# The last normalisation of a two-layer streaming encoder: mean taken off first, weight and bias last

## The chip, the cores and the metric

The kernel runs on one core of one Trainium2 chip. The core has a matrix engine (PE, with its weight loads shown as PEld), a vector engine (DVE), a scalar engine (ACT), a third elementwise engine (POOL, GpSimd) and a queue engine (SP), which issues most transfers. The metric is the time of one execution in microseconds of device time. Less is better. Before the change the median of three runs is 2924.94 us (2924.41 to 2925.33).

## The reference

One inference step of a two-layer encoder over 256 prompt frames and 32 sample frames, 288 together, each of 2048 channels. Layer 0 mixes tokens by a gated MLP, layer 1 by retention; after each comes a SwiGLU feed-forward. Every sublayer ends in a residual and a normalisation over the 2048 channels of a frame. The change touches the very last of the four:

```python
def layer_norm(x, g, b):
    xf = x.astype(jnp.float32)
    mu = jnp.mean(xf, axis=-1, keepdims=True)
    var = jnp.mean(jnp.square(xf - mu), axis=-1, keepdims=True)
    y = (xf - mu) * lax.rsqrt(var + LN_EPS) * g.astype(jnp.float32) + b.astype(jnp.float32)
    return y.astype(x.dtype)

def trunk(x, ...):
    for i in range(DEPTH):
        ...
        x = layer_norm(ALPHA * x + h, ln_mix_g[i], ln_mix_b[i])
        x = layer_norm(ALPHA * x + swiglu(x, w_ffn_in[i], w_ffn_out[i]), ln_ffn_g[i], ln_ffn_b[i])
    return x, ...
```

## The kernel before

Activations are held transposed: a tile is 128 channels (partitions) by 288 frames, and `y` has KT = 16 such tiles side by side. Weights come in blocks of 128 by 128, eight to a chunk of 512 KB, on SP's queue; ACT and DVE split every chunk into a rounded part and the rest (`split`, lines 363 to 365), and PE makes three products for each block (`step`, lines 91 to 98). The blocks follow one another in the order in which PE uses them. PE's order is the order of the program; the other engines' instructions are put in order by a scheduler when the kernel is built.

The last feed-forward ends with 16 output tiles, one after the other, 22 blocks each. When one is done, `PostNorm.last` (line 210) adds it to `y` on DVE (line 215). A rough mean `c`, taken from the first tile in `center`, is subtracted from every tile (line 252), so that the later squares stay small. `sums` (line 250) squares the tile on ACT (line 254) and adds tile and square to two running sums on DVE (lines 257 and 258). For the last normalisation (`self.out` is set) it also multiplies the tile by its weight on ACT (line 264).

The 16th tile isn't added to the sums: `stats` (line 266) multiplies the sums (line 275) and the last tile and its square (line 278) by a constant matrix of 1/2048 on PE, which leaves the mean `m1` and the mean square `m2` of every frame in two PSUM banks, on all partitions alike. Then come, one after the other: the weight of the last tile (281), the square of the mean (285), the variance `v` (286), a first value of its inverse root by Ln and Exp (292, 293), one Newton step of three instructions on DVE (`newton`, lines 165 to 168), which gives the factor `a`, its copy into a PSUM bank `ap` (296), and the offset `b = -mean * a` (297).

After that the tiles are finished in pairs. `scale` (line 301) multiplies a pair by the factor, on DVE with `ap`, or on POOL with `a` for pairs 4 and 10. `shift` (line 305) forms on ACT, for each tile, `b` times the weight plus the bias in a buffer `wide` (line 308), and adds the two to the pair, on DVE or POOL (line 309). Eight stores of a pair each, 288 KB, follow on SP's queue in the order 0, 2, 6, 4, 8, 12, 10, 14 (line 322); each waits until its pair is done.

Buffers: PSUM has four banks for products (`acc`) and four others (`aux`); SBUF has three buffers for incoming weight chunks (tag `raw`).

Of the kernel before, what the change touches and what calls it, by code (L numbers as in the profile page):

```python
# [8 lines left out]

F32 = mybir.dt.float32  # L10
F32R = mybir.dt.float32r
I32 = mybir.dt.int32
AF = mybir.ActivationFunctionType
ALU = mybir.AluOpType
PSUM = bass.MemoryType.PSUM
PE = mybir.EngineType.PE

P = 128
D = 2048
KT = D // P  # L20
NP = 256
NS = 32
NT = NP + NS
# [9 lines left out]
LN_EPS = 1e-5  # L33
GN_EPS = 1e-6
CB = 8
# [7 lines left out]
class Core:  # L43
# [47 lines left out]
    def step(self, ps, w, k, m, x, first, last):  # L91
        mm = self.nc.tensor.matmul
        hi, lo = self.blk(w, k, m)
        xh, xl = x
        n = xh.shape[-1]
        mm(ps[:, :n], hi, xh, start=first, stop=False)  # L96
        mm(ps[:, :n], hi, xl, start=False, stop=False)  # L97
        mm(ps[:, :n], lo, xh, start=False, stop=last)  # L98
# [59 lines left out]
def rsqrt(nc, out, v, t):  # L158

    nc.vector.tensor_scalar(out.bitcast(I32), v.bitcast(I32), -0.5, float(0x5F3759DF), ALU.mult, ALU.add)  # L160
    for _ in range(3):
        newton(nc, out, out, v, t)


def newton(nc, out, r, v, t):
    nc.vector.scalar_tensor_tensor(t, r, -0.5, r, ALU.mult, ALU.mult)
    nc.vector.tensor_tensor(t, t, v, ALU.mult)
    nc.vector.scalar_tensor_tensor(out, t, 1.5, r, ALU.add, ALU.mult)


class PostNorm:
# [38 lines left out]
    def last(self, m, ps, first_part=False):  # L210
        nc, lnp, gi = self.nc, self.lnp, self.gi
        if first_part:
            self.part(m, ps)
        else:
            nc.vector.tensor_tensor(self.y[:, m, :], ps[:, :NT], self.y[:, m, :], ALU.add)
        if self.n == 0:
            self.s = lnp.tile([P, 2, NT], F32, tag="sums", name=f"sums{gi}")
            nc.gpsimd.memset(self.s, 0.0)
            if self.out is not None:
                self.core.tc.keep_in_program_order(nc.scalar.preload_act_table_set("natural_log_exp_and_others"))  # L220
            else:
                gb = self.cst["ln"][:, gi, :, :].rearrange("p a k -> p k a")
                nc.scalar.copy(self.xh[:, :, NT:], gb)
                nc.vector.tensor_tensor(self.xl[:, :, NT:], gb, self.xh[:, :, NT:].bitcast(F32), ALU.subtract)
            r = self.tmp("cen", F32R)
            nc.scalar.copy(r, self.y[:, m, :])
            self.core.after(2, lambda: self.center(r))
        self.n += 1
        if self.c is None:
            self.wait.append(m)  # L230
        else:
            self.sums(m)
        if self.n == KT:
            if self.out is None:
                self.parts = [[self.tmp(f"s{i}{j}", F32R) for j in range(2)] for i in range(2)]
                for i, (hi, lo) in enumerate(self.parts):
                    split(nc, hi, lo, self.s[:, i, :])
            self.core.after(1 if self.out is not None else 2, lambda: self.stats(m))

    def center(self, r):  # L240

        nc = self.nc
        ps = self.core.bank(f"cen{self.gi}")
        nc.tensor.matmul(ps[:, :NT], self.cst["one_r"], r, start=True, stop=True)
        self.c = self.lnp.tile([P, NT], F32, tag="cen", name=f"cens{self.gi}")
        nc.scalar.mul(self.c, ps[:, :NT], float(KT))
        for q in self.wait:
            self.sums(q)

    def sums(self, m):  # L250
        nc, d = self.nc, self.y[:, m, :]
        nc.vector.tensor_tensor(d, d, self.c, ALU.subtract)
        sq = self.tmp(f"sq{m}")
        nc.scalar.activation(sq, d, AF.Square)
        self.sq = sq
        if self.n < KT or self.out is None:
            nc.vector.tensor_tensor(self.s[:, 0, :], self.s[:, 0, :], d, ALU.add)
            nc.vector.tensor_tensor(self.s[:, 1, :], self.s[:, 1, :], sq, ALU.add)
        if self.out is None:
            g = self.gain(m)  # L260
            nc.scalar.mul(self.xh[:, m, :NT], d, g)
            nc.vector.scalar_tensor_tensor(self.xl[:, m, :NT], d, g, self.xh[:, m, :NT].bitcast(F32), ALU.mult, ALU.subtract)
        elif self.n < KT:
            nc.scalar.mul(d, d, self.gain(m))

    def stats(self, m):
        nc, core, gi = self.nc, self.core, self.gi
        one = self.cst["one2048"]
        st = [core.bank(f"m{i}_{gi}") for i in range(2)]
        for i in range(2):  # L270
            if self.out is None:
                for j, r in enumerate(self.parts[i]):
                    nc.tensor.matmul(st[i][:, :NT], self.cst["one_r"], r, start=j == 0, stop=j == 1)
            else:
                nc.tensor.matmul(st[i][:, :NT], one, self.s[:, i, :], start=True, stop=False)
        if self.out is not None:
            for i, r in enumerate((self.y[:, m, :], self.sq)):
                nc.tensor.matmul(st[i][:, :NT], one, r, start=False, stop=True)
        m1, m2 = st[0][:, :NT], st[1][:, :NT]
        if self.out is not None:  # L280
            nc.scalar.mul(self.y[:, m, :], self.y[:, m, :], self.gain(m))
        v, t = self.tmp("v"), self.tmp("t")
        self.a = a = self.lnp.tile([P, NT], F32, tag="a", name=f"a{gi}")
        self.b = b = self.lnp.tile([P, NT], F32, tag="b", name=f"b{gi}")
        nc.scalar.activation(t, m1, AF.Square)
        nc.vector.scalar_tensor_tensor(v, m2, LN_EPS, t, ALU.add, ALU.subtract)
        if self.out is None:
            rsqrt(nc, a, v, t)
            nc.vector.scalar_tensor_tensor(b, m1, -1.0, a, ALU.mult, ALU.mult)
            return  # L290
        r = self.tmp("r")
        nc.scalar.activation(t, v, AF.Ln)
        nc.scalar.activation(r, t, AF.Exp, scale=-0.5)
        ap = core.bank("ap")[:, :NT]
        newton(nc, a, r, v, t)
        nc.scalar.copy(ap, a)
        nc.vector.scalar_tensor_tensor(b, m1, -1.0, a, ALU.mult, ALU.mult)
        pool = (4, 10)
        row = lambda k: self.y[:, k:k + 2, :]

        def scale(k):
            eng, f = (nc.gpsimd, a) if k in pool else (nc.vector, ap)
            eng.tensor_tensor(row(k), row(k), f.unsqueeze(1).broadcast_to([P, 2, NT]), ALU.mult)

        def shift(k):
            u = self.wide(k // 2)
            for i in range(2):
                nc.scalar.activation(u[:, i, :], b, AF.Identity, bias=self.bias(k + i), scale=self.gain(k + i))
            (nc.gpsimd if k in pool else nc.vector).tensor_tensor(row(k), row(k), u, ALU.add)

        for k in pool:
            scale(k)
        ks = [k for k in range(0, KT, 2) if k not in pool]
        scale(ks[0])
        for k, nxt in zip(ks, ks[1:] + [None]):
            if nxt is not None:
                scale(nxt)
            shift(k)
            if k in (2, 8):
                shift(k + 2)  # L320
        for k in (0, 2, 6, 4, 8, 12, 10, 14):
            nc.sync.dma_start(self.out[:, k:k + 2, :], row(k))

    def norm(self, k):
        nc, d = self.nc, self.y[:, k:k + 2, :]
# [37 lines left out]
def split(nc, hi, lo, f):  # L363
    nc.scalar.copy(hi, f)  # L364
    nc.vector.tensor_tensor(lo, f, hi.bitcast(F32), ALU.subtract)  # L365
# [426 lines left out]
def hybrid_step(ctx, tc, ins, outs):  # L792
    nc = tc.nc
    ctx.enter_context(tc.manual_schedule(engines={PE}))
    core = Core(ctx, tc, ins["wpack"])
# [112 lines left out]
```

## Time and profile before

| what | value |
|---|---|
| median of three runs | 2924.94 us |
| the profiled execution, its own time | 2923.75 us |
| its span, first to last instruction | 2922.0 us |
| mean granted clock of PE | 0.997 |
| PE busy | 99% of the span |
| DVE, ACT, POOL busy | 59%, 43%, 5% |
| start of the last product of the feed-forward | 2900.84 us |
| first store of the result issued | 2910.34 us |
| last store issued | 2918.49 us |
| a store, from issue to landing | 2.1 to 2.6 us, median 2.3 |

All times of the trace are microseconds from the first instruction. A row of the timeline gives start, duration, engine, line, operation, what is written and read with shapes, a count where equal rows are merged, and in brackets how long the engine stood idle before and what ended that. A row of a group gives busy time and the mean duration of one in ns, and the idle time before. A duration holds the whole life of one instruction; where the next doesn't depend on it, it may start some tenths of a microsecond before that ends, so that the distance of two starts is what a row of such instructions costs.

### The profile page before, as it was taken

The numbers are of one execution on the slowest core, as the hardware profiler recorded it, in microseconds if no ns is written. First come the engines' busy times: TensorE is split into PE (matmuls) and PEld (weight loads), VectorE is DVE, ScalarE is ACT, GpSimd is POOL, SyncE is SP. The second block draws the span as 40 slices with busy tenths as digits, with TensorE's granted clock in tenths as the row PEclk, the third lists the DMA queues.
The fourth block names the chain that finished last, engine by engine and source line by source line (L and its number), as shares of the span: only waits on it lengthen the run. The fifth ranks groups of instructions, "written<-read, shape, count | busy, mean of one in ns | idle before, by whom it ended". The sixth has DMA issues, their size and how long they took to land.

```text
span 2922.0 us, 51538 instructions
## 1 busy us (share of the span) xinstructions
PE 2899.8 (99%) x21576; PEld 2885.3 (99%) x21576; DVE 1712.9 (59%) x2489; ACT 1256.8 (43%) x1676; POOL 141.6 (5%) x236
## 2 busy tenths in 40 slices
PE   9999999999999999999999999999999999999997
PEld 9999999999999999999999999999999999999997
DVE  5667865444444456787755566767864444444455
ACT  5444544333333344564443344445553333333344
POOL 1100000000000000012200111200000000000000
PEclk9999999999999999999999999999999999999998
DMA  8644445555544545557654566655545554455553
GB/s 281 211 161 159 159 166 166 166 165 163 165 165 166 166 159 169 187 185 233 223 185 166 185 214 202 222 183 166 160 158 173 166 166 163 164 165 166 166 166 112
DMA packets 147161, 516.16 MB, mean 177 GB/s; under 512 B 18080, under 2 KB 21168, under 8 KB 146768
## 3 DMA queue, kind: packets, MB, share of 16 engines
q1 hardware_dynamic: 132704, 474.28, 49.3%
q0 software_dynamic: 14224, 38.59, 4.4%
q8 instruction: 169, 2.77, 0.4%
q14 instruction: 64, 0.52, 0.1%
HBM read 487.63 MB, written 25.17 MB: 175 GB/s over the span
## 4 chain that ended last, share of the span: by engine, by line
PE 98%; DVE 1%; ACT 0%; DMA 0%; SPq 0%; issue 0%; DVEq 0%; ACTq 0%
PE af_in L97 13%; PE af_in L96 13%; PE af_in L98 13%; PE ab_in L97 7%; PE ab_in L96 7%; PE ab_in L98 7%; PE af_out L96 6%; PE af_out L98 6%; PE af_out L97 6%; PE ab_out L98 2%; PE ab_out L96 2%; PE ab_out L97 2%; PE aa_in L96 2%; PE aa_in L97 2%; PE aa_in L98 2%; PE aa_out L96 1%
## 5 line engine op out<-in xcount | busy, mean ns | idle before, releaser
L365 DVE TENSOR_TENSOR wlo<-raw,whi 128x1024 fp32r<-128x1024 f32 (+1 forms) x894 | 1085.9, 1216 | 937.3 <-ACT whi L364 933.3
L364 ACT CAST whi<-raw 128x1024 fp32r<-128x1024 f32 (+1 forms) x894 | 931.1, 1043 | 1479.9 <-PE af_in L97 370.5
L97 PE MATMUL af_in<-xl,whi 128*128 128x288 f32 (+1 forms) x2816 | 833.0, 296 | 0.0
L96 PE MATMUL af_in<-xh,whi 128*128 128x288 f32 (+1 forms) x2816 | 832.9, 296 | 0.0
L98 PE MATMUL af_in<-xh,wlo 128*128 128x288 f32 (+1 forms) x2816 | 831.8, 295 | 0.0
L97 PEld LDWEIGHTS af_in<-xl,whi 128*128 128x128 f32 x2816 | 532.1, 189 | 0.0
L98 PEld LDWEIGHTS af_in<-xh,wlo 128*128 128x128 f32 x2816 | 531.6, 189 | 0.0
L96 PEld LDWEIGHTS af_in<-xh,whi 128*128 128x128 f32 x2816 | 531.1, 189 | 0.0
L97 PE MATMUL ab_in<-xl,whi 128*128 128x288 f32 (+1 forms) x1536 | 454.4, 296 | 0.7 <-DVE xl L365 0.7
L96 PE MATMUL ab_in<-xh,whi 128*128 128x288 f32 (+1 forms) x1536 | 454.9, 296 | 0.0
L98 PE MATMUL ab_in<-xh,wlo 128*128 128x288 f32 (+1 forms) x1536 | 453.6, 295 | 0.0
L96 PE MATMUL af_out<-hh,whi 128*128 128x288 f32 x1408 | 416.0, 295 | 0.0
L97 PE MATMUL af_out<-hl,whi 128*128 128x288 f32 x1408 | 415.1, 295 | 0.0
L98 PE MATMUL af_out<-hh,wlo 128*128 128x288 f32 x1408 | 414.4, 294 | 0.0
L97 PEld LDWEIGHTS ab_in<-xl,whi 128*128 128x128 f32 x1536 | 290.3, 189 | 2.0 <-DVE xl L365 0.9
L96 PEld LDWEIGHTS ab_in<-xh,whi 128*128 128x128 f32 x1536 | 289.6, 189 | 1.0
L98 PEld LDWEIGHTS ab_in<-xh,wlo 128*128 128x128 f32 x1536 | 289.9, 189 | 0.0
L98 PEld LDWEIGHTS af_out<-hh,wlo 128*128 128x128 f32 x1408 | 264.9, 188 | 0.0
L97 PEld LDWEIGHTS af_out<-hl,whi 128*128 128x128 f32 x1408 | 264.2, 188 | 0.0
L96 PEld LDWEIGHTS af_out<-hh,whi 128*128 128x128 f32 x1408 | 263.9, 187 | 0.0
L96 PE MATMUL aa_in<-xh,whi 128*128 128x288 f32 x512 | 152.7, 298 | 1.1 <-ACT whi L364 1.1
L98 PE MATMUL aa_in<-xh,wlo 128*128 128x288 f32 x512 | 151.5, 296 | 0.7 <-DVE wlo L365 0.7
(237 smaller groups left out, 2976.6 us busy)
## 6 DMA issues: line engine op xcount, KB each, us to landing
raw<-in_wpack_dram SPq DMA_DIRECT2D x886, 512.0 KB, 3.4
v_room<-tv POOLq DMA_DIRECT2D x32, 144.0 KB, 4.7
of<-o_room POOLq DMA_DIRECT2D x32, 144.0 KB, 4.5
vw<-v_room POOLq DMA_DIRECT2D x8, 512.0 KB, 5.4
out_st_s_dram<-sso POOLq DMA_DIRECT2D x16, 256.0 KB, 2.8
out_st_p_dram<-so POOLq DMA_DIRECT2D x16, 256.0 KB, 5.3
o_room<-to POOLq DMA_DIRECT2D x8, 512.0 KB, 3.8
y<-in_xT_dram SPq DMA_DIRECT2D x8, 288.0 KB, 6.7
```

The lines of the kernel that those rows point to most:

```text
L96: mm(ps[:, :n], hi, xh, start=first, stop=False)
L97: mm(ps[:, :n], hi, xl, start=False, stop=False)
L98: mm(ps[:, :n], lo, xh, start=False, stop=last)
L364: nc.scalar.copy(hi, f)
L365: nc.vector.tensor_tensor(lo, f, hi.bitcast(F32), ALU.subtract)
```

## The change

Only the last normalisation changes. The multiplication of each tile by its weight in the loop (264 and 281) goes. When the 15th tile has come (`last`, n = 15), a buffer of tag `raw` is taken for two matrices of 128 by 128: an identity, made on POOL, and one that is -1 in its first row and 0 elsewhere. The rough mean is subtracted from tile 15 then, before its last product is added. The two sums over the first 15 tiles are split into a rounded part and the rest, and are multiplied by the rounded constant matrix on PE.

What follows the statistics is a new function, `finish`, in an order written out by hand for DVE, ACT and POOL; SP's queue is still put in order by the scheduler. ACT copies the mean into SBUF. The mean is taken off first: on PE for tiles 6, 7, 12 and 13 (an identity product of the tile plus one of the -1 row with the mean, in four PSUM banks `off`), on POOL for pairs 4, 8 and 10, on DVE for pairs 0, 2 and 14. `v` and the Newton step lie in PSUM banks, and the factor ends in `ap` without a copy; a copy of it goes to SBUF as `a`. The tiles are scaled by it, on POOL for its pairs, else on DVE. Weight and bias come last, in one instruction for each tile: on DVE for tiles 10, 11, 13, 14 and 15, on ACT for the others. Tile 12 is stored singly on ACT's queue and tile 13 singly on SP's; the others go in pairs.

```diff
@@ last
+        if self.out is not None and self.n == KT - 1:
+            room = self.core.wp.tile([P, CB * P], F32, tag="raw", name="centring", bufs=3)
+            self.ident, self.minus = room[:, :P], room[:, P:2 * P]
+            make_identity(nc, self.ident)
+            nc.gpsimd.memset(self.minus, 0.0)
+            nc.gpsimd.memset(self.minus[:1, :], -1.0)
+            d = self.y[:, KT - 1, :]
+            nc.vector.tensor_tensor(d, d, self.c, ALU.subtract)
...
+        if self.n == (KT if self.out is None else KT - 1):
+            self.parts = [[self.tmp(f"s{i}{j}", F32R) for j in range(2)] for i in range(2)]
+            for i, (hi, lo) in enumerate(self.parts):
+                split(nc, hi, lo, self.s[:, i, :])
@@ sums
-        nc.vector.tensor_tensor(d, d, self.c, ALU.subtract)
+        if self.out is None or self.n < KT:
+            nc.vector.tensor_tensor(d, d, self.c, ALU.subtract)
...
-        elif self.n < KT:
-            nc.scalar.mul(d, d, self.gain(m))
@@ stats
-                nc.tensor.matmul(st[i][:, :NT], one, self.s[:, i, :], start=True, stop=False)
+            for j, r in enumerate(self.parts[i]):
+                nc.tensor.matmul(st[i][:, :NT], self.cst["one_r"], r, start=j == 0, stop=j == 1 and self.out is None)
...
-            nc.scalar.mul(self.y[:, m, :], self.y[:, m, :], self.gain(m))
...
+    def finish(self, m1, m2):
+        nc, core, a, mean = self.nc, self.core, self.a, self.b
+        mm = nc.tensor.matmul
+        ap = core.bank("ap")[:, :NT]
+        v = core.accum("fin")[:, :NT]
+        t, r = self.tmp("t"), self.tmp("r")
+        pool = (4, 8, 10)
+        copied = (6, 7, 12, 13)
+        late = (10, 11, 13, 14, 15)
+        row = lambda k: self.y[:, k:k + 2, :]
+        off = {k: (core.bank if i == 3 else core.accum)(f"off{k}")[:, :NT] for i, k in enumerate(copied)}
+
+        def pair(k, op, vec, gp):
+            eng, f = (nc.gpsimd, gp) if k in pool else (nc.vector, vec)
+            eng.tensor_tensor(row(k), row(k), f.unsqueeze(1).broadcast_to([P, 2, NT]), op)
+
+        center = lambda k: pair(k, ALU.subtract, m1, mean)
+
+        def scale(k):
+            if k in copied:
+                for i in (k, k + 1):
+                    nc.vector.tensor_tensor(self.y[:, i, :], off[i], a, ALU.mult)
+            else:
+                pair(k, ALU.mult, ap, a)
+
+        def affine(k, n=2, queue=None):
+            for i in range(k, k + n):
+                d = self.y[:, i, :]
+                if i in late:
+                    nc.vector.tensor_scalar(d, d, self.gain(i), self.bias(i), ALU.mult, ALU.add)
+                else:
+                    nc.scalar.activation(d, d, AF.Identity, bias=self.bias(i), scale=self.gain(i))
+            (queue or nc.sync).dma_start(self.out[:, k:k + n, :], self.y[:, k:k + n, :])
+
+        with core.tc.manual_schedule(engines=FINISH):
+            nc.scalar.activation(t, m1, AF.Square)
+            nc.scalar.copy(mean, m1)
+            for k in copied:
+                mm(off[k], self.ident, self.y[:, k, :], start=True, stop=False)
+                mm(off[k], self.minus, mean, start=False, stop=True)
+            for k in pool:
+                center(k)
+            nc.vector.scalar_tensor_tensor(v, m2, LN_EPS, t, ALU.add, ALU.subtract)
+            nc.scalar.activation(t, v, AF.Ln)
+            nc.scalar.activation(r, t, AF.Exp, scale=-0.5)
+            center(0)
+            nc.vector.scalar_tensor_tensor(ap, v, -0.5, r, ALU.mult, ALU.mult)
+            nc.vector.tensor_tensor(ap, ap, r, ALU.mult)
+            nc.vector.scalar_tensor_tensor(ap, ap, 1.5, r, ALU.add, ALU.mult)
+            scale(0)
+            nc.scalar.copy(a, ap)
+            for k in pool:
+                scale(k)
+            center(2)
+            affine(0)
+            scale(6)
+            affine(6)
+            scale(2)
+            affine(4)
+            affine(2)
+            center(14)
+            scale(12)
+            affine(8)
+            scale(14)
+            affine(14)
+            affine(10)
+            affine(12, 1, nc.scalar)
+            affine(13, 1)
```

The removed part of `stats` and the old functions `scale` and `shift` with their loop are in the listing above.

More of the change, by code (lines that the diff above doesn't have):

```diff
@@ L8 @@
 from concourse._compat import with_exitstack
+from concourse.masks import make_identity
 F32 = mybir.dt.float32
@@ L16 @@
 PE = mybir.EngineType.PE
+FINISH = {mybir.EngineType.DVE, mybir.EngineType.Activation, mybir.EngineType.Pool}
 P = 128
@@ L232, in last @@
             self.sums(m)
+        if self.n == (KT if self.out is None else KT - 1):
+            self.parts = [[self.tmp(f"s{i}{j}", F32R) for j in range(2)] for i in range(2)]
+            for i, (hi, lo) in enumerate(self.parts):
+                split(nc, hi, lo, self.s[:, i, :])
         if self.n == KT:
[L234 to L237, printed above, removed]
             self.core.after(1 if self.out is not None else 2, lambda: self.stats(m))
@@ L270, in stats @@
         for i in range(2):
[L271 to L274, printed above, removed]
-                nc.tensor.matmul(st[i][:, :NT], one, self.s[:, i, :], start=True, stop=False)
+            for j, r in enumerate(self.parts[i]):
+                nc.tensor.matmul(st[i][:, :NT], self.cst["one_r"], r, start=j == 0, stop=j == 1 and self.out is None)
         if self.out is not None:
@@ L279, in stats @@
         m1, m2 = st[0][:, :NT], st[1][:, :NT]
-        if self.out is not None:
-            nc.scalar.mul(self.y[:, m, :], self.y[:, m, :], self.gain(m))
-        v, t = self.tmp("v"), self.tmp("t")
         self.a = a = self.lnp.tile([P, NT], F32, tag="a", name=f"a{gi}")
         self.b = b = self.lnp.tile([P, NT], F32, tag="b", name=f"b{gi}")
+        if self.out is not None:
+            self.finish(m1, m2)
+            return
+        v, t = self.tmp("v"), self.tmp("t")
         nc.scalar.activation(t, m1, AF.Square)
@@ L286, in stats @@
         nc.vector.scalar_tensor_tensor(v, m2, LN_EPS, t, ALU.add, ALU.subtract)
[L287 to L293, printed above, removed]
-        ap = core.bank("ap")[:, :NT]
-        newton(nc, a, r, v, t)
-        nc.scalar.copy(ap, a)
-        nc.vector.scalar_tensor_tensor(b, m1, -1.0, a, ALU.mult, ALU.mult)
@@ L298, in stats @@
-        pool = (4, 10)
-        row = lambda k: self.y[:, k:k + 2, :]
-        def scale(k):
[L302 to L322, printed above, removed]
+        rsqrt(nc, a, v, t)
+        nc.vector.scalar_tensor_tensor(b, m1, -1.0, a, ALU.mult, ALU.mult)
```

## The prediction

> **What bounds the kernel now.** I read the page first, for the share of each engine, then the timeline of the last 22 us, then the chain of waits there, then busy time and DMA by single microseconds, and last the groups by form for prices. The page says that PE is the bound almost to the end:
>
> ```profile
> span 2922.0 us, 51538 instructions
> PE 2899.8 (99%) x21576; PEld 2885.3 (99%) x21576; DVE 1712.9 (59%) x2489; ACT 1256.8 (43%) x1676; POOL 141.6 (5%) x236
> ```
>
> What is not PE's is the last normalisation, from PE's last product (end 2901.15 in the chain) to 2922.0: 20.85 us. Only there can this change act. The timeline of it (start, duration, engine, line):
>
> ```profile
> 2900.84 0.29 PE L98 MATMUL af_out<-hh,wlo 128*128 128x288 f32 x1
> ...
> 2901.67 0.46 DVE L252 TENSOR_TENSOR y<-y,cens 128x288 f32<-128x288 f32 x1
> ...
> 2903.03 0.53 ACT L281 ACTIVATE y<-y,lnv 128x288 f32<-128x288 f32 x1 [0.43 <-PE m L278]
> 2903.47 0.39 ACT L285 ACTIVATE t<-m 128x288 f32<-128x288 f32 x1
> 2903.90 0.46 DVE L286 SCALAR_TENSOR_TENSOR v<-m,t 128x288 f32<-128x288 f32 x1 [1.77 <-ACT t L285]
> ...
> 2906.32 0.46 DVE L168 SCALAR_TENSOR_TENSOR a<-t,r 128x288 f32<-128x288 f32 x1
> 2906.82 0.40 ACT L296 COPY ap<-a 128x288 f32<-128x288 f32 x1 [1.51 <-DVE a L168]
> ...
> 2906.93 2.76 POOL L303 TENSOR_TENSOR y<-y,a 128x576 f32<-128x576 f32 x2 [844.27 <-DVE a L168]
> 2907.25 1.42 DVE L303 TENSOR_TENSOR y<-y,ap 128x576 f32<-128x576 f32 x2
> 2907.31 8.40 ACT L308 ACTIVATE wide<-b,lnv 128x288 f32<-128x288 f32 x16
> 2908.59 1.72 DVE L309 TENSOR_TENSOR y<-y,wide 128x576 f32<-128x576 f32 x1
> ```
>
> Up to 2907 it is a chain of single small instructions. Then ACT makes sixteen `wide` terms in 8.40 us (0.525 each, start to start), and DVE follows. DVE's L303, with one operand in PSUM, takes 0.74 although POOL runs beside it; its L309, with both operands in SBUF, took 1.72 and ended 0.62 after POOL's two instructions did (2909.69). The stores close it; by microsecond (engines, PE clock, DMA share, GB/s):
>
> ```profile
> 2916.00:2917.00 1.00, 0.00 (x0) 0.00 (x0) 1.00 (x2) 0.00 (x0) 0.00 (x0) 0.50 0.33 129
> 2917.00:2918.00 1.00, 0.00 (x0) 0.00 (x0) 1.00 (x3) 0.00 (x0) 0.00 (x0) 0.50 1.04 394
> 2918.00:2919.00 1.00, 0.00 (x0) 0.00 (x0) 0.46 (x1) 0.00 (x0) 0.00 (x0) 0.50 1.00 380
> 2919.00:2920.00 1.00, 0.00 (x0) 0.00 (x0) 0.00 (x0) 0.00 (x0) 0.00 (x0) 0.50 1.01 392
> 2920.00:2921.00 1.00, 0.00 (x0) 0.00 (x0) 0.00 (x0) 0.00 (x0) 0.00 (x0) 0.50 0.46 180
> ```
>
> The last five stores, issued from 2915.82 to 2918.49, move without a gap until 2920.47 (quarter-microsecond windows): 288 KB at 390 GB/s is 0.755 us each. From issue to first data is 0.83; from last data to the end of the span 1.53.
>
> **The change, part by part.**
>
> *Inside the loop.* Fifteen L264 multiplications leave ACT, one 0.46 subtraction moves ahead, two splits (ACT 0.43, DVE 0.45 each) and POOL's identity are added. All lie under PE: DVE is idle for 6.88 us before L215, and POOL's tile is free once the third-last weight split ends (2884.15), 18 us before its use. Zero; uncovered, the splits would cost 1.8.
>
> *To v.* L252 (0.49 with its gap) leaves the path, and L281 goes, which held ACT 0.44 before L285. The four products of the split sums take 0.13 each instead of 1.13 together, so PE is free in time. v starts at 2903.90 - 0.93 = 2902.97.
>
> *To the first scale.* Ln and Exp keep 0.47 each: r at 2904.37. The subtraction for tile 0 (0.74) is put on DVE ahead of Newton; between v's end (2903.43) and r it fits with 0.2 to spare; uncovered it costs 0.67. Newton is three times 0.49. It now writes PSUM from DVE, which no row here shows: reading PSUM costs nothing extra (L215 455 ns, L257 in SBUF 454), ACT's copy to PSUM 403; I take 0 of a range from -0.1 to +0.4. The copy into `ap` (0.43) goes. Scaling starts at 2904.41 + 1.47 = 2905.88 instead of 2907.25.
>
> *ACT afterwards.* In the built program the copy of `a` waits for DVE and the weights behind it no more, so I take that wait to be for DVE's scale of pair 0 (ended 2906.62): copy 0.40, and ACT starts weights and biases at 2907.02. There are eleven, not sixteen, in place; the same form stands in the loop:
>
> ```profile
> L330 ACT ACTIVATE y<-y,lnv 128x288 f32<-128x288 f32 x48 | 27.3, 620 | 6.8 <-DVE y L327 6.8
> L160 DVE TENSOR_SCALAR a<-v 128x288 int32<-128x288 int32 x3 | 0.9, 310 | 0.1
> ```
>
> At 0.525 each: pair 0 stored from 2908.16, pair 8 complete at 2912.36, tile 12 at 2912.89.
>
> *POOL.* Now three subtractions and three scalings of 1.38: from the copied mean (2903.3, start 2903.42) to 2911.70 without a pause, because `a` is there at 2907.05. Before, POOL's two pairs ended at 2915.18.
>
> *PE.* Eight products for four tiles; two of that kind (L275) took 1.13, so 0.565 each, 4.5 us from 2903.0 to 2907.5. They are wanted from 2907.2 (tile 6) to 2909.7 (tile 13), at least 2 us after each is made. Nothing is behind them.
>
> *DVE.* From 2905.88 five pairs at 0.67 and four single tiles at 0.37: 4.83, so tile 14 is ready for its weight at 2910.78. Weight and bias of 14, 15, 10, 11 and 13 are tensor_scalar between SBUF, form of L160: 0.31 for 288 elements, where a two-operand instruction needs 0.46. Whether POOL holds such a one up no row shows; the bounds are no hold (14 done at 2911.4) and L309's full hold until POOL ends. I take the hold, 14 and 15 done at 2912.32, since the short time speaks for two reads at once; 13 is done at 2913.25.
>
> [...]
>
> *Stores.* Nine instead of eight. SP's queue was reordered: 0, 6, 4, 2, 14, 8, 10, 13; pair 8 is thus behind 14, and 14 behind POOL. Tile 12 goes out from ACT, which has issued no store here: SP's issue is 0.33 to 0.43, POOL's 0.51 to 0.76; either leaves it inside the stream. From 14's issue (2912.35) first data at 2913.18, then three pairs and two single tiles, 4 x 0.755 = 3.02: 2916.20.
>
> **Sum.** Last data 2916.20 instead of 2920.47: 4.27 less; the 1.53 after it stay. Span 2917.7. The profiled execution took 2923.75 (span plus 1.75) and would take 2919.5. The median of the runs is 2924.94, so 1.2 above it; less 4.27 gives 2920.7.
>
> **Rivals.**
>
> *The stores stream without a gap.* If ACT's pairs came as fast as the data, the 6.04 us of data would run from 2908.99 to 2915.03: 5.44 less, 2919.5, the most that the store rate allows. For it: in the old trace the last five do so. Against: ACT gives a pair every 1.05. Runs differ by 0.9, so such a gain may measure up to 6.3.
>
> *PE's clock falls.* The old windows show 1.00 to 2906 and 0.50 from 2907, with PE idle. If the eight products ran at half, 9.0 us, tile 13 would come at 2912.0; 14 is behind it on DVE and stored 1.4 later: 2922.1. Against: PE is not idle here until 2907.
>
> *POOL holds DVE throughout (slower).* POOL is busy without pause from 2903.4 to 2911.7, just where DVE does its part. If instructions with one PSUM operand were held as L309 was, each costs 1.0 more. Five lie before the first scale is out: `a` comes at 2912.05, POOL ends at 2916.2, stored data ends at 2920.7: that is the point where the gain is gone. With the seven further instructions behind them DVE is 12 late, data ends at 2927.2, and the time is 2931.7. Against: L303's 0.74 beside POOL.
>
> **How the numbers follow.** Forecast 0.57 (own range 2919.6 to 2922.0), gapless stores 0.25, PE's clock 0.12, POOL's hold 0.06. Within 0.2% is about what a measurement of this kernel can tell from no change, here 5.85 us. Faster than that: about 0.15 of the gapless case and 0.08 of the forecast's early end, 0.23. Slower: most of the last case, 0.05. The rest 0.72. The range reaches from the gapless case less 0.9 (2918.6) to PE's clock with the PSUM bound of Newton, 0.4, and some of the runs' difference (2923.0).
>
> **What would show it.** First scale near 2905.9 and DVE's three Newton rows at 0.46: the chain. Eleven Identity rows end to end on ACT: its pace. Tensor_scalar rows of 14 that start before and end after POOL's last: the hold. `off` products done before 2908: PE. DMA full from 2913.2 to 2916.2: the end. Wrong would be: DVE rows of 1.7 beside POOL, a gap in POOL's six, or stores landing later than 2.6 after issue.

## The result

The changed kernel takes 2919.80 us (median of 21 runs, 2918.72 to 2921.53); the kernel before, in 21 runs beside it, takes 2924.41 us (2923.25 to 2928.63). The ratio is 0.9984 with a 95% interval of 0.9978 to 0.999: some 4.6 us less, or 0.16%. That is clear of no change, but the interval, 0.10 to 0.22%, reaches across the 0.2% that the prediction takes as the least difference. The forecast was 2920.7, range 2918.6 to 2923.0.

The page of the changed kernel, span and busy times:

```profile
span 2917.0 us, 51551 instructions
PE 2903.5 (100%) x21592; PEld 2887.8 (99%) x21592; DVE 1709.3 (59%) x2493; ACT 1247.6 (43%) x1658; POOL 145.1 (5%) x242
```

The span is 5.0 us shorter, but not all of that is the change. In the first 20 us PE waits for its first split weights; that wait was 1.1 us in the profiled execution before and 0.4 in the one after, in code that the change doesn't touch, and the addition of the 16th tile (L215 before, L217 after) starts at 2900.61 instead of 2901.18. In the fourteen traces of this study that start lies anywhere from 2900.61 to 2903.29, in no relation to the edits. So I compare a *tail*: from the start of that addition to the end of the span. It is 20.82 us before and 16.39 after, 4.43 less; 4.42 of it is gained by the time the last stored data have moved. Each kernel has one trace, and spans are printed to a tenth of a microsecond, so I read nothing into a tenth.

The timeline of that tail in the changed kernel (start, duration, engine, line, operation; what the engine waited for in brackets). Its clock runs 0.57 ahead of the old one, so 0.57 is added where it is set against the prediction:

```profile
2900.61 0.46 DVE L217 TENSOR_TENSOR y<-af_out,y 128x288 f32<-128x288 f32 x1 [5.92 <-PE af_out L100]
...
2902.51 0.47 DVE L341 SCALAR_TENSOR_TENSOR fin<-m,t 128x288 f32<-128x288 f32 x1 [1.44 <-PE m L284]
2902.76 4.13 POOL L313 TENSOR_TENSOR y<-y,b 128x576 f32<-128x576 f32 x3 [17.97 <-ACT b L335]
...
2904.43 0.47 DVE L346 TENSOR_TENSOR ap<-ap,r 128x288 f32<-128x288 f32 x1
2904.93 0.47 DVE L347 SCALAR_TENSOR_TENSOR ap<-ap,r 128x288 f32<-128x288 f32 x1
...
2905.43 0.75 DVE L313 TENSOR_TENSOR y<-y,ap 128x576 f32<-128x576 f32 x1
...
2906.22 0.40 ACT L349 COPY a<-ap 128x288 f32<-128x288 f32 x1 [2.32 <-DVE y L313]
2906.51 5.81 ACT L330 ACTIVATE y<-y,lnv 128x288 f32<-128x288 f32 x11
```

The first scale starts 4.82 us into the tail, where it was 6.07 before: 1.25 of the gain is in the chain of small instructions. ACT then has eleven instructions in a row instead of sixteen. DVE's L313, with one operand in PSUM, took 0.75 while POOL ran and was not held: the same form, L303 in the old trace, took 0.75 beside POOL (at 2907.25) and 0.74 with POOL idle (at 2912.61 and 2916.39). The L328, DVE's five weights, have no such operand, and this is their group (count, then least, median and longest duration in ns):

```profile
L328 DVE TENSOR_SCALAR y<-y,lnv x5: 417/418/834, 2910.3 to 2912.1; 128x288 f32<-128x288 f32 x5
```

The 834 is the first, which began while POOL's last scaling ran (to 2911.00) and ended at 2911.17. The stores, by single microseconds (busy engines, PE's clock, then DMA share and GB/s in the last two columns):

```profile
2911.00:2912.00 1.00, 0.00 (x0) 0.00 (x0) 1.00 (x4) 1.00 (x3) 0.00 (x0) 0.50 0.77 295
2912.00:2913.00 1.00, 0.00 (x0) 0.00 (x0) 0.53 (x2) 0.32 (x1) 0.00 (x0) 0.50 1.04 389
...
2915.00:2916.00 1.00, 0.00 (x0) 0.00 (x0) 0.00 (x0) 0.00 (x0) 0.00 (x0) 0.50 0.51 178
```

Up to 2912 the first four pairs move at 295 GB/s or less in any of these windows, against 372 to 395 in the three from 2912 to 2915. Pair 14 is issued at 2911.53, and from its data on the DMA is full (a share of 1.00 to 1.08 in those three) until 2915.52, the last data. The end of the span follows 1.48 later, as before (1.49, read in the same way).

### The profile page after: what moved, and what is told of

Read it like the earlier page. It is cut to its first block, busy times and chain, and to the rows that moved or that the text cites. A ratio compares the mean times of both kernels' runs of the same rounds, so it can differ in the third digit from the quotient of the medians.

```text
span 2917.0 us, 51551 instructions
## 1 busy us (share of the span) xinstructions
PE 2903.5 (100%) x21592; PEld 2887.8 (99%) x21592; DVE 1709.3 (59%) x2493; ACT 1247.6 (43%) x1658; POOL 145.1 (5%) x242
## 4 chain that ended last, share of the span: by engine, by line
PE 99%; DVE 1%; DMA 0%; SPq 0%; ACT 0%; issue 0%; DVEq 0%; ACTq 0%
PE af_in L99 13%; PE af_in L98 13%; PE af_in L100 13%; PE ab_in L99 7%; PE ab_in L98 7%; PE ab_in L100 7%; PE af_out L98 6%; PE af_out L100 6%; PE af_out L99 6%; PE ab_out L100 2%; PE ab_out L99 2%; PE ab_out L98 2%; PE aa_in L98 2%; PE aa_in L100 2%; PE aa_in L99 2%; PE aa_out L98 1%
```

## The experiments

Twelve kernels, each with five rounds against the kernel before and a trace of its own. Their medians lie between 2919.69 and 2922.89 us and their intervals overlap, since the start scatters as much as the edits are worth; only the tail of the trace, one for each kernel, tells them apart. Each edit is one of the changed kernel.

| edit | median us | ratio to before (95%) | tail us | against 16.39 |
|---|---|---|---|---|
| none (the changed kernel) | 2919.80 | 0.9984 (0.9978 to 0.999) | 16.39 | |
| keep_mul | 2919.69 | 0.9983 (0.9974 to 0.9992) | 16.31 | -0.08 |
| late_c | 2921.27 | 0.9986 (0.9977 to 0.9995) | 16.91 | +0.52 |
| sbuf_newton | 2922.89 | 0.9991 (0.9983 to 1.0) | 18.49 | +2.10 |
| no_pe | 2921.90 | 0.9987 (0.9978 to 0.9996) | 17.51 | +1.12 |
| act_all | 2920.96 | 0.9986 (0.9977 to 0.9995) | 17.57 | +1.18 |
| half_store | 2919.98 | 0.9983 (0.9974 to 0.9991) | 15.24 | -1.15 |
| pool_two | 2921.03 | 0.9986 (0.9977 to 0.9994) | 16.62 | +0.23 |
| all_sp | 2920.82 | 0.9985 (0.9976 to 0.9994) | 16.31 | -0.08 |
| sbuf_pool4 | 2922.50 | 0.9991 (0.9982 to 1.0) | 18.06 | +1.67 |
| copy_first | 2919.97 | 0.9985 (0.9976 to 0.9993) | 16.50 | +0.11 |
| psum14 | 2920.17 | 0.9986 (0.9977 to 0.9995) | 16.62 | +0.23 |
| psum14_copy | 2919.77 | 0.9983 (0.9974 to 0.9992) | 16.76 | +0.37 |

**keep_mul: the removed multiplications in the loop, put back as idle work.**

```diff
             nc.vector.scalar_tensor_tensor(self.xl[:, m, :NT], d, g, self.xh[:, m, :NT].bitcast(F32), ALU.mult, ALU.subtract)
+        elif self.n < KT:
+            nc.scalar.mul(self.xl[:, m, :NT], d, self.gain(m))
```

> The fifteen weight multiplications of the loop are put back on ACT, into a tile that nobody reads. My theory (the gain lies wholly after the last product): as the changed kernel, 0 within 0.3 us, and the stretch from the last product to the end keeps 16.4 us. Rival (a lighter ACT in the loop lets PE run earlier, which would explain why PE's last product came 0.57 us earlier in the changed kernel's trace): 0.5 us slower, and that product 0.5 us later, with the waits of PE in the loop longer.

Measured -0.08 in the tail, which is nothing. The tail can't show what happens in the loop; the windows of the stretch with the multiplications do, for the changed kernel and for keep_mul (PE, PEld, DVE, ACT and POOL busy, then the columns as above):

```profile
2500.00:2900.00 400.00, 400.00 (x3008) 400.00 (x3007) 192.89 (x228) 149.64 (x183) 1.07 (x4) 1.00 0.49 158
2500.00:2900.00 400.00, 400.00 (x3008) 400.00 (x3007) 193.81 (x228) 156.31 (x200) 1.06 (x4) 1.00 0.46 159
```

ACT has 6.7 us more to do, and PE is busy without a gap in both, with the same 3008 products. The tail of keep_mul starts 1.4 us later, but 1.0 of that is the wait for the first split weights again (1.4 instead of 0.4), and 0.2 a later wait for DVE's split. So fifteen instructions taken from ACT under PE's bound bought no time.

**late_c: tile 15's rough mean is subtracted after its last product again.**

```diff
-            d = self.y[:, KT - 1, :]
-            nc.vector.tensor_tensor(d, d, self.c, ALU.subtract)
...
-        if self.out is None or self.n < KT:
-            nc.vector.tensor_tensor(d, d, self.c, ALU.subtract)
+        nc.vector.tensor_tensor(d, d, self.c, ALU.subtract)
```

> The rough mean is subtracted from tile 15 after its last product again. My theory: everything behind starts 0.49 us later, POOL and ACT too, and the end comes 0.49 us later. Rival (the end is set by the rate of the stores, and the chain has slack before them): 0 to 0.1 us.

Measured +0.52: the instruction costs its row and gap (0.46 long, and `v` starts 2.40 us into the tail instead of 1.90), and everything behind it is that much later. The chain is exposed from its first instruction on.

**sbuf_newton: the Newton step in SBUF again, and the copy into `ap` after it.**

```diff
-            nc.vector.scalar_tensor_tensor(ap, v, -0.5, r, ALU.mult, ALU.mult)
-            nc.vector.tensor_tensor(ap, ap, r, ALU.mult)
-            nc.vector.scalar_tensor_tensor(ap, ap, 1.5, r, ALU.add, ALU.mult)
+            nc.vector.scalar_tensor_tensor(a, v, -0.5, r, ALU.mult, ALU.mult)
+            nc.vector.tensor_tensor(a, a, r, ALU.mult)
+            nc.vector.scalar_tensor_tensor(a, a, 1.5, r, ALU.add, ALU.mult)
+            nc.scalar.copy(ap, a)
             scale(0)
-            nc.scalar.copy(a, ap)
```

> Newton's three instructions write SBUF, and ACT copies the factor to PSUM ahead of the first scale. My theory as it stood on record: the copy is 0.43 us on the path, so the end comes 0.4 us later. Rival (after the trace: what counts is when ACT starts its weights; with the factor in PSUM ACT's copy waits for the first scale, with it in SBUF it doesn't): the first scale 0.43 us later, but ACT's first weight only 0.14 us later and tile 14 held by POOL as before, so the end 0 to 0.15 us later.

Measured +2.10, and neither theory stands. The timeline of this kernel (the tail starts at 2901.61):

```profile
2903.76 4.34 POOL L313 TENSOR_TENSOR y<-y,b 128x576 f32<-128x576 f32 x3 [17.96 <-ACT b L335]
...
2905.42 1.43 DVE L346 TENSOR_TENSOR a<-a,r 128x288 f32<-128x288 f32 x1
2906.89 1.54 DVE L347 SCALAR_TENSOR_TENSOR a<-a,r 128x288 f32<-128x288 f32 x1
2908.46 0.40 ACT L348 COPY ap<-a 128x288 f32<-128x288 f32 x1 [3.56 <-DVE a L347]
...
2908.89 0.76 DVE L313 TENSOR_TENSOR y<-y,ap 128x576 f32<-128x576 f32 x1 [0.47 <-ACT ap L348]
```

Two instructions with both inputs in SBUF take 1.43 and 1.54 us, where the changed kernel's rows took 0.47, and POOL's three subtractions take 4.34 instead of 4.13. By themselves these three are (ns, least, median, longest):

```profile
L313 POOL TENSOR_TENSOR y<-y,b x3: 1400/1410/1612, 2903.8 to 2906.5; 128x576 f32<-128x576 f32 x3
```

In these rows the two engines take turns: DVE's L346 started during POOL's second subtraction (which ended at 2906.54) and ended 0.3 behind it; POOL's third, next in its row, was 0.2 longer than the other two; and L347 ended 0.3 behind that one. DVE's first Newton row, with `fin` in PSUM as one input, ran beside POOL too and took 0.46. By which mechanism the engines hold each other no row shows.

The first scale starts 7.28 us into this tail instead of 4.82, 2.46 later: 2.04 of that are the two rows, 0.42 the copy. ACT's weights start only 2.17 later, since ACT's copy no longer stands behind the first scale, and the tail grows by about as much.

**sbuf_pool4: the same, with POOL given pair 4 alone, so that it is idle during Newton.** Pairs 8 and 10 go to DVE; the Newton lines are those of sbuf_newton and left out here.

```diff
-        pool = (4, 8, 10)
+        pool = (4,)
...
+            center(8)
+            scale(8)
             scale(12)
...
             affine(14)
+            center(10)
+            scale(10)
             affine(10)
```

> Newton in SBUF again, but POOL has only pair 4 (one subtraction of 1.38 us, over at about 2904.2 on the after trace's clock, before Newton's second instruction); pairs 8 and 10 go to DVE with their PSUM operand. Theory (POOL's subtractions held Newton): its second and third instruction take 0.47 us again instead of 1.43 and 1.54, the first scale is out some 0.4 us behind the after kernel's (the copy) and not 2.1, and the first tensor_scalar takes 0.42 us. DVE has four more pair instructions (3.0 us), two of them behind tile 15, so the tail from the last evacuation to the end of the span is about 17.7 us (after 16.4, sbuf_newton 18.5). Rival (an in-place Newton in SBUF is slow by itself): the rows stay at 1.4 to 1.5 us and the tail is 19.7 us or more.

The timeline of this kernel (the tail starts at 2901.24):

```profile
2905.05 0.46 DVE L346 TENSOR_TENSOR a<-a,r 128x288 f32<-128x288 f32 x1
2905.54 0.46 DVE L347 SCALAR_TENSOR_TENSOR a<-a,r 128x288 f32<-128x288 f32 x1
```

The same two instructions take 0.46 each. The first scale starts 5.23 into the tail, 0.41 later than in the changed kernel, which is the copy, and the tail is 18.06 where 17.7 was expected, for DVE's four more pair instructions. That settles it: Newton in SBUF is not slow by itself; it was slow, 1.43 and 1.54, where POOL ran beside it.

**no_pe: tiles 6, 7, 12 and 13 get their mean taken off on DVE.**

```diff
-        copied = (6, 7, 12, 13)
+        copied = ()
...
+            center(6)
             scale(6)
...
             center(14)
+            center(12)
             scale(12)
```

> The mean of tiles 6, 7, 12 and 13 is taken off by DVE in pairs instead of PE. My theory (DVE's and ACT's work after the factor counts): DVE gets 2 x 0.67 more and 0.12 less, ACT waits 0.6 us for tile 6, and the last data lands 0.8 us later. Rival (the stores or POOL set the end alone): 0 to 0.2 us.

Measured +1.12. ACT's wait for tile 6, from its waits in the tail (what waited, for what: total, times, longest),

```profile
ACT y L330 <- DVE y L313: 0.7, 1, 0.7
```

shows how the two further DVE instructions reach the stores: by ACT's pace first, and by tiles 14 and 15 later, which are done 12.0 us into the tail instead of 10.9. The scheduler also put pair 8 ahead of pair 14 on SP's queue here, but that pair was issued at 12.1, hardly behind them, so the turn explains less than 0.1 of the 1.12. The loss is more than the 0.8 expected. PE's eight products take work from DVE where DVE has no time to spare.

**act_all: all sixteen weights and biases on ACT.**

```diff
-        late = (10, 11, 13, 14, 15)
+        late = ()
```

> All sixteen weight-and-bias instructions are on ACT. My theory (ACT's pace of 0.525 us was one of the bounds): ACT ends 5 x 0.525 = 2.6 us later, which leaves the stores drained before it, and the last data lands 0.8 to 1.1 us later than in the changed kernel. Rival (the store stream sets the end whatever comes before): 0 to 0.2 us.

Measured +1.18. From this kernel's timeline (the tail starts at 2901.43):

```profile
2907.32 7.88 ACT L330 ACTIVATE y<-y,lnv 128x288 f32<-128x288 f32 x15
...
2915.66 0.63 ACT L330 ACTIVATE y<-y,lnv 128x288 f32<-128x288 f32 x1 [0.46 <-ACT y L330]
```

ACT's fifteenth ends 13.8 us into the tail, by which time the changed kernel's last store has been on its way for more than a microsecond. Not all of the 1.18 is the five weights, though: between the fifteenth and the sixteenth, tile 13's, ACT issues the store of tile 12, which holds tile 13's weight up by 0.46. With that store on SP's queue the loss might be up to 0.46 less; that was not run.

**half_store: of pairs 14, 8 and 10 only the first tile is stored.**

```diff
+            w = 1 if k in (14, 8, 10) else n
-            (queue or nc.sync).dma_start(self.out[:, k:k + n, :], self.y[:, k:k + n, :])
+            (queue or nc.sync).dma_start(self.out[:, k:k + w, :], self.y[:, k:k + w, :])
```

> Of the pairs 14, 8 and 10 only the first tile is stored; tiles 15, 9 and 11 are left out of the output. My theory (the last five stores wait for one another, 3.02 us of data from tile 14's on): 1.13 us of data less, and tile 13's own issue becomes the bound, so the end comes 1.2 us earlier. Rival (the end is set by when the last tile is ready, plus a fixed landing): 0 to 0.2 us earlier.

Measured -1.15 for 432 KB less, which at the 0.755 us of a 288 KB pair are 1.13. From pair 14 on, the rate of the transfers sets the end.

**pool_two: pair 8 goes from POOL to DVE.**

```diff
-        pool = (4, 8, 10)
+        pool = (4, 10)
...
+            center(8)
+            scale(8)
+            affine(8)
             scale(12)
-            affine(8)
             scale(14)
```

> Pair 8 goes from POOL to DVE. My theory: POOL ends 1.5 us earlier and holds no tensor_scalar any more (all five at 0.42), DVE gets 1.34 us more, tile 14 is ready 0.5 us later but pair 8 is stored ahead of it; the end comes 0.2 us later. Rival (POOL's hold of tile 14 sets the end): the end 0.4 us earlier.

Measured +0.23. POOL is done before DVE comes to the L328, and the group has no long one any more:

```profile
L328 DVE TENSOR_SCALAR y<-y,lnv x5: 423/424/429, 2914.5 to 2915.8; 128x288 f32<-128x288 f32 x5
```

The hold on tile 14's weight (834 ns in the changed kernel, 423 to 429 here) is POOL's, as predicted, and worth less than the pair that POOL carries.

**all_sp: tiles 12 and 13 as one store on SP.**

```diff
-            affine(12, 1, nc.scalar)
-            affine(13, 1)
+            affine(12)
```

> Tiles 12 and 13 are stored as one pair on SP's queue, as the last. My theory (the bytes in the stream set the end): 0 within 0.15 us. Rival (a store on a queue of its own, or in single tiles, brings a gain): 0.4 us later, by one more issue behind the others.

Measured -0.08, nothing: inside this full stream neither the queue nor the cut of the last pair mattered.

**copy_first, psum14, psum14_copy: the two limits ahead of the last four stores.** The first puts ACT's copy of `a` ahead of the first scale, so that ACT may start earlier. The second gives tiles 14 and 15 to PE instead of 12 and 13 and leaves them in PSUM until their weight, so that POOL may not hold it. The third does both.

The edit of copy_first:

```diff
+            nc.scalar.copy(a, ap)
             scale(0)
-            nc.scalar.copy(a, ap)
```

The edit of psum14:

```diff
-        copied = (6, 7, 12, 13)
+        copied = (6, 7, 14, 15)
...
-                    nc.vector.tensor_tensor(self.y[:, i, :], off[i], a, ALU.mult)
+                    nc.vector.tensor_tensor(off[i] if i > 12 else self.y[:, i, :], off[i], a, ALU.mult)
...
-                    nc.vector.tensor_scalar(d, d, self.gain(i), self.bias(i), ALU.mult, ALU.add)
+                    nc.vector.tensor_scalar(d, off.get(i, d), self.gain(i), self.bias(i), ALU.mult, ALU.add)
...
-            center(14)
+            center(12)
```

> ACT's copy of a stands ahead of DVE's scale of pair 0 and no longer waits for it. Theory: ACT's weights start 0.3 us earlier (they then wait for the scale itself), the first four stores go out 0.3 us earlier, and the tail stays at 16.4 us (within 0.1), because the last four stores' data start with pair 14, whose issue hangs on DVE's tensor_scalar held by POOL. Rival (ACT's pace sets the end): tail 16.1 us.

> PE takes the mean off tiles 14 and 15 instead of 12 and 13, DVE's scale leaves them in PSUM, and their tensor_scalar reads PSUM and writes SBUF. Theory (the hold comes with SBUF input at the fast form): both take 0.47 us with no hold although POOL runs, so pair 14 is issued 0.25 us earlier; the data of pair 2 before it end only at 2912.37 on the after trace's clock, where pair 14's data start already, so the tail falls by 0 to 0.15 us (16.25 to 16.4). Rival (POOL's port holds the write as well): the first takes 0.8 us, the second 0.47, pair 14 is 0.05 us later, tail 16.45 us.

> Both edits together: pair 2 is 0.3 us and pair 14 0.25 us earlier. Theory (two limits of almost the same height, both have to go): tail 16.1 us, 0.25 us less than the after kernel's, where each edit alone gives 0.15 us at most. Rivals: one of the two sets the end by itself (then that edit alone gives the same), or the stores' issue on SP does (then none of the three moves the tail).

Measured +0.11, +0.23 and +0.37: no gain in any. In copy_first (tail from 2901.00) the wait only changed sides:

```profile
2905.81 0.40 ACT L348 COPY a<-ap 128x288 f32<-128x288 f32 x1 [1.53 <-DVE ap L347]
2906.24 0.76 DVE L313 TENSOR_TENSOR y<-y,ap 128x576 f32<-128x576 f32 x1 [0.46 <-ACT a L348]
```

In the changed kernel the copy waited for the scale, here the scale waits for the copy, though both only read `ap`: in both programs the second reader started 0.03 to 0.04 after the first had ended. Whether the two could read `ap` side by side no run tried. DVE's whole sequence is thus 0.42 later, ACT's 0.13, and the first L328, which comes to POOL's end anyway, starts only 0.23 before that and takes 0.43, so there is hardly anything left to hold; pair 14 is issued at the same point of the tail, 10.9, and the tail stays.

In psum14 the group of L328 shows the hold gone but the instruction slower:

```profile
L328 DVE TENSOR_SCALAR y<-off,lnv x2: 567/568/568, 2912.5 to 2913.0; 128x288 f32<-128x288 f32 x2
```

568 ns from PSUM instead of 418 from SBUF (0.47 was expected), and no 834. Tiles 14 and 15 were done 10.8 into the tail, a tenth earlier than in the changed kernel. The gain was thrown away elsewhere: SP's queue is ordered by the scheduler, which now put pair 8 ahead of pair 14: SP waits five times for ACT's L330, where it did four times in the changed kernel. Pair 8 was issued when ACT had it, 11.3 into the tail, and the stream of the last four began 0.3 later. So the two limits were not tested as meant: whether both edits with pair 14 kept in front would gain the quarter microsecond is open. No kernel of this study that stores the whole result beats the changed one by more than a tenth of a microsecond in the tail.

## Why the prediction was right

The mechanism of the forecast is what happened, and most of its steps stand to within 0.16 us. All measured times have the 0.57 added:

| step | predicted | measured |
|---|---|---|
| `v` starts | 2902.97 | 2903.08 |
| `r` done | 2904.37 | 2904.46 |
| first scale | 2905.88 | 2906.00 |
| PE's eight products done | 2907.5 | 2907.03 |
| ACT's weights start | 2907.02 | 2907.08 |
| ACT done with tile 12 | 2912.89 | 2912.89 |
| POOL done | 2911.70 | 2911.57 |
| pair 14 issued | 2912.35 | 2912.10 |
| tile 13 done | 2913.25 | 2913.09 |
| last data | 2916.20 | 2916.09 |

*To the first scale.* `v` starts 0.11 later than predicted because it waits for the mean square (the row's bracket names PE's L284), not for ACT. keep_mul, by PE's windows, and late_c confirm the two prices, nothing for the loop and half a microsecond for L252. Newton in PSUM took 0.47 a row against 0.46: the zero inside "-0.1 to +0.4" was right.

*What that edit is worth was not seen.* The prediction credits the Newton step with the copy's 0.43 only. sbuf_newton shows 2.10, five times as much: with Newton in SBUF, POOL's earlier start holds two of its instructions for 1.0 each, and sbuf_pool4, where POOL is idle then, has both at 0.46. The price of the new form was right, that of the old form in the new order was missing. The rival of a hold throughout had the hold and its limit (rows with an operand in PSUM were not held); it was refuted for the same reason that made Newton's move pay (0.47 a row in PSUM), and L313 at 0.74 to 0.75 beside POOL is the row that refutes it.

*The last tiles.* Two terms were mis-sized and partly cancel. A tensor_scalar costs 0.34 start to start and not 0.31, and five of them 0.15 more. The hold, taken as a full 0.31 behind POOL's end, left only 0.17 of the instruction to do (ended 2911.17, POOL 2911.00); with POOL itself 0.13 earlier, pair 14 was issued 0.25 earlier. That the hold exists, for which no row of the old trace spoke, was right: 834 ns beside POOL, 423 to 429 without it in pool_two, and 567 with its input in PSUM beside POOL in psum14. The reason that the prediction gives for the hold, that the short time speaks for two reads at once, no row shows.

*The stores.* Four times 0.755 from pair 14's first data was predicted; 2911.53 + 0.83 + 3.02 gives 2915.38 on the new clock, and 2915.52 was measured. half_store shows that the rate is the limit there. The rival of gapless stores fell: the first four pairs moved at 295 GB/s and less, because ACT gives a pair every 1.05. The rival of PE's clock fell too, since the clock stood at 1.00 until 2909.75, 3.3 us after PE's last product.

*A sign that misled.* The prediction would have called itself wrong if stores landed later than 2.6 us after their issue. Three did: pair 10 after 3.1, tile 12 after 2.8 and tile 13 after 3.0. The sign was at odds with the prediction's own sum, in which tile 13 is issued at 2913.25 at the earliest and the last data move at 2916.20, 2.95 later: these three stood behind others in a full stream and landed late without anything being wrong. The other two signs, DVE rows of 1.7 beside POOL and a gap in POOL's six, did not appear.

*The sum.* The tail lost 4.43 where 4.27 was forecast. The forecast of the time, 2920.7, lies 0.9 above the median: 0.53 of that is the median of the runs before (2924.94 in three, 2924.41 in twenty-one), 0.16 the tail, and 0.2 lies within what single runs differ by. The chance of 0.72 for "within 0.2%" met a change of 0.16%; with an interval that reaches to 0.22%, the side on which it fell is in part luck.

*Part by part.* With the others in place, the mean of four tiles on PE is worth 1.1, five weights on DVE 0.7 to 1.2, Newton in PSUM 2.1, tile 15's early subtraction 0.5, POOL's third pair 0.2, and the single stores nothing. These do not add up to 4.43, and need not: each is measured with the rest as it is, and several relieve the same DVE.

## What to carry to other kernels

When a new order makes two engines run side by side that did not before, price the old form of each instruction beside its new neighbour, not only the new form: what Newton's place in PSUM saved here up to the first scale was above all DVE's turns behind POOL, 2.0 us, and only then the copy, 0.4. Before moving one instruction to relieve a limit, look at every queue that a scheduler orders by itself; a store queue that turned round took more than the edit gave in psum14, 0.3 us against a tenth. Where the start of a kernel scatters by more than an edit is worth, measure the edit in its own stage of the trace, from a point that no edit touches.

## What the runs showed of the hardware

With two SBUF inputs, DVE's instructions and POOL's held each other up one by one and in both directions in sbuf_newton: DVE's 0.46 (in sbuf_pool4, with POOL idle) became 1.43 and 1.54, and POOL's 1.40 became 1.61 in between. With one input in PSUM, DVE's L313 stayed at 0.75 beside POOL in the changed kernel. A float32 tensor_scalar of 288 elements took 0.42 us from SBUF (changed kernel) but 0.57 from PSUM (psum14), 0.34 and 0.49 from start to start. So beside POOL the input in PSUM saved 0.27 against the row that POOL held (0.83 in the changed kernel), and it cost 0.15 against the rows that POOL did not hold.
